# Moving the pieces of the modulation rows between the stages of a transformer layer on one core

## The chip, the cores and the metric

The kernel runs on one core of a Trainium2 chip. The metric is the time of one execution on the device in microseconds (us); the time before is the median of three runs. Engines are named as the profile names them: PE is TensorE's matmul, PEld its weight load, DVE is VectorE, ACT is ScalarE, POOL is GpSimd, and SP is SyncE, whose instruction stream issues nearly all loads.

## What is computed

One layer of a diffusion backbone: 256 latent tokens and 256 context tokens of width 2048, all in float32. Cut to what matters here:

```
m_lat = split(silu(c) @ w_ada + b_ada, 6)          # 6 modulation rows of 2048
m_ctx = split(silu(c_ctx) @ w_ada + b_ada, 6)      # of which 0 and 1 are used
h  = rms_norm(x,   norm1_g) * (1 + m_lat[1]) + m_lat[0]
hc = rms_norm(ctx, norm1_g) * (1 + m_ctx[1]) + m_ctx[0]
p, pc = h @ w_in, hc @ w_in[:, :3072]              # q, k, v and two gates; k, v alone for ctx
oa = grouped-query attention(rope(q_a), k_a, v_a)  # latent queries, all keys
ob = differential attention(rope(q_b), k_b, v_b)
merged = sigmoid(g_a) * (oa @ w_br_a) + sigmoid(g_b) * (ob @ w_br_b)
x1 = x + m_lat[2] * (merged @ w_out)
h2 = rms_norm(x1, norm2_g) * (1 + m_lat[4]) + m_lat[3]
out = x1 + m_lat[5] * ((silu(h2 @ w_ff_gate) * (h2 @ w_ff_up)) @ w_ff_down)
```

Rows 0 and 1 of the modulation are made early by matmuls (`ada_cond`). Rows 2, 4 and 3 (the gate, scale and shift around the second norm) and row 5 are made on VectorE in pieces, and the change concerns the first three of these.

## The kernel before

**Matmuls in three parts.** Weights and activations are split into a high and a low half. A weight tile is 128 x 2 x 512 (512 KB): SP loads it into a `wraw` buffer (seven of them), ScalarE casts it to `whi` (L235), VectorE makes `wlo` = raw - high (L237); three `whi` and three `wlo` buffers exist. `mm3` then issues activation-high by `whi` (L241), activation-high by `wlo` (L242) and activation-low by `whi` (L243). All engines run their instructions in the order in which they stand.

**Stages.** The projection to keys and values is done in channel steps, `STEPS = ((0, 1), (1, 1), (2, 2), (4, 4), (8, 4), (12, 4))`: first channel tile and number of channel tiles. The document names a step by its entry. Each step takes six column groups of 512; a group of the last three steps has two halves of one weight tile and 24 matmuls each, and at its end VectorE adds the four tokens' results to the sum in SBUF (L443). The last group of a step is `va` (column group 1). While a step runs, `ada_cond` makes rows 0 and 1 of the modulation for the next step: its weight pieces (`ada_t`) are loaded into `wraw` and other buffers (L295, L300, L304), and TensorE multiplies them in bursts (L315). `modulated` then makes the next step's activations: a product on VectorE (`hx`, L357), the high half on ScalarE (L360), the low half on VectorE (L361).

Then come the attention (q projections, gates, one branch projection, both attentions, woven together), the merge (`w_br_a`, 32 weight tiles), the output projection (`w_out`, 32 tiles), the feed-forward part.

**The pieces.** `ada_later` makes rows 2, 4 and 3, one after the other, each from 32 pieces: SP loads 512 KB of `w_ada` into a `wraw` buffer (L453), and VectorE multiplies it by the condition and adds it to an accumulator (L458 for the first two, L460 for the others). The accumulate of a piece is issued when the next piece is taken, and stands behind the last `wlo` issued by then. After 32 pieces four small matmuls sum the accumulator over the partitions (`adac`, L474), VectorE adds the bias (L475; for the scale it multiplies by `norm2_g`, L477), and POOL writes the row to DRAM (L478). `take(later, n)` takes n pieces; where these calls stand decides beside which work the pieces run. In the projection they stand in the loop over groups and halves, in the attention in `side_work`, which is called once per weight tile, in the merge after each of the last four weight tiles of a column group.

The order of instructions on an engine is settled when the program is built: a scheduler takes them by priority, which is the order of the code, and by when it thinks that their inputs and buffers are ready.

## Time and profile before

| what | value |
|---|---|
| median of three runs | 1694.38 us (1694.19 to 1694.4) |
| the profiled execution, its own time | 1696.49 us |
| its span, first to last instruction | 1694.7 us |
| mean granted clock of TensorE | 0.999 |
| VectorE: `wlo` (L237) | 607.0 us in 498 instructions |
| VectorE: pieces (L460, all rows) | 152.1 us in 120 instructions |
| HBM read | 395.35 MB, 243 GB/s over the span with writes |

A row of the timeline gives the start in us, the duration, engine, line, operation, what is written from what, the count, and in brackets how long the engine idled before it and who ended that. A row of a stretch gives its bounds, its length, the busy time of PE, PEld, DVE, ACT and POOL with their counts, the granted clock, the DMA share and GB/s. A row of the waits gives who waited for whom: us in total, times, the longest. On TensorE a matmul of 512 columns lasts 0.39 us, while the next one starts 0.23 us after it.

### The profile page before, as it was taken

To read this page: it belongs to the slowest core of one execution; us is meant where nothing else is said; L and a number is where in the kernel's file an instruction comes from. 1 tells how busy PE (TensorE), PEld (TensorE's weight loads), DVE (VectorE), ACT (ScalarE), POOL (GpSimd) and SP (SyncE) were. 2 spreads that over 40 slices of the span, in tenths; PEclk is the share of its full clock that TensorE was granted. 3 is DMA by queue.
4 is the path that set the end of the run, shared out by engine and by line. 5 is a ranking of instruction groups with operands and counts; after the bars stand their busy time and mean duration, and the time that the engine had idled before them with its cause. 6 is when DMAs were issued, how large, how long until landed. Compare 5 with 4: busy or idle time off the path is not lost.

```text
span 1694.7 us, 21499 instructions
## 1 busy us (share of the span) xinstructions
PE 1675.7 (99%) x7889; PEld 1354.8 (80%) x7889; DVE 1143.0 (67%) x1454; ACT 776.4 (46%) x1055; POOL 202.3 (12%) x296
## 2 busy tenths in 40 slices
PE   7999999999999999999999999999999999999998
PEld 5677778887887778888888888888888888888887
DVE  5765779697798888986666755566666666544454
ACT  5231222246666566667544534444444444333332
POOL 0200002011131110011111101111111111100000
PEclk9999999999999999999999999999999999999999
DMA  9888875777767767766877857888888898866662
GB/s 349 300 311 286 299 256 169 237 249 257 231 198 228 247 208 256 265 228 201 266 257 248 293 171 215 250 258 263 266 265 268 263 277 253 240 216 197 214 208 88
DMA packets 181284, 413.08 MB, mean 244 GB/s; under 512 B 15001, under 2 KB 16234, under 8 KB 180922
## 3 DMA queue, kind: packets, MB, share of 16 engines
q1 hardware_dynamic: 168906, 374.17, 67.3%
q0 software_dynamic: 12272, 37.53, 7.4%
q8 instruction: 62, 1.02, 0.3%
q14 instruction: 44, 0.36, 0.1%
HBM read 395.35 MB, written 16.29 MB: 243 GB/s over the span
## 4 chain that ended last, share of the span: by engine, by line
PE 92%; DVE 3%; DMA 2%; ACT 1%; issue 1%; POOL 0%; SPq 0%; DVEq 0%; ACTq 0%; POOLq 0%
PE mm L242 28%; PE mm L241 28%; PE mm L243 28%; PE ada L315 2%; PE ptp L815 1%; DVE wlo L237 1%; PE s L791 1%; PE mm L402 1%; PE o L836 1%; DMA wada<-in_ada_t_dram 1%; DMA wraw<-in_w_ff_gate_dram 0%; ACT whi L235 0%; DMA gate_d<-gate 0%; DMA wraw<-in_w_in_dram 0%; DVE ada L460 0%
## 5 line engine op out<-in xcount | busy, mean ns | idle before, releaser
L237 DVE TENSOR_TENSOR wlo<-wraw,whi 128x1024 fp32r<-128x1024 f32 x498 | 607.0, 1220 | 425.1 <-ACT whi L235 423.8
L235 ACT CAST whi<-wraw 128x1024 fp32r<-128x1024 f32 x498 | 522.8, 1051 | 727.1 <-PE mm L243 624.0
L242 PE MATMUL mm<-wlo,hT 128*128 128x512 f32 x684 | 266.2, 389 | 0.4 <-DVE wlo L237 0.4
L243 PE MATMUL mm<-whi,hT 128*128 128x512 f32 x684 | 266.1, 389 | 0.0
L241 PE MATMUL mm<-whi,hT 128*128 128x512 f32 x684 | 266.1, 389 | 0.0
L241 PE MATMUL mm<-whi,xT 128*128 128x512 f32 x630 | 251.9, 402 | 0.0
L242 PE MATMUL mm<-wlo,xT 128*128 128x512 f32 x630 | 247.3, 393 | 2.7 <-DVE wlo L237 2.7
L243 PE MATMUL mm<-whi,xT 128*128 128x512 f32 x630 | 246.8, 392 | 0.0
L460 DVE SCALAR_TENSOR_TENSOR ada<-wada,vt,ada 128x1024 f32<-128x1024 f32 x120 | 152.1, 1278 | 0.0
L242 PEld LDWEIGHTS mm<-wlo,hT 128*128 128x128 f32 x684 | 128.4, 188 | 27.7 <-DVE wlo L237 0.9
L241 PEld LDWEIGHTS mm<-whi,hT 128*128 128x128 f32 x684 | 128.4, 188 | 26.8
L243 PEld LDWEIGHTS mm<-whi,hT 128*128 128x128 f32 x684 | 128.4, 188 | 26.4
L241 PEld LDWEIGHTS mm<-whi,xT 128*128 128x128 f32 x630 | 118.2, 188 | 33.0 <-issue 6.6
L242 PEld LDWEIGHTS mm<-wlo,xT 128*128 128x128 f32 x630 | 118.8, 189 | 27.6 <-DVE wlo L237 5.0
L243 PEld LDWEIGHTS mm<-whi,xT 128*128 128x128 f32 x630 | 118.5, 188 | 25.8 <-DVE xT L361 0.3
L241 PE MATMUL mm<-whi,fT 128*128 128x512 f32 x354 | 137.5, 388 | 0.5 <-DVE y L1128 0.5
L242 PE MATMUL mm<-wlo,fT 128*128 128x512 f32 x354 | 137.3, 388 | 0.0
L243 PE MATMUL mm<-whi,fT 128*128 128x512 f32 x354 | 137.3, 388 | 0.0
L241 PEld LDWEIGHTS mm<-whi,fT 128*128 128x128 f32 x354 | 66.4, 188 | 15.0 <-issue 0.8
L243 PEld LDWEIGHTS mm<-whi,fT 128*128 128x128 f32 x354 | 66.4, 188 | 13.8
L242 PEld LDWEIGHTS mm<-wlo,fT 128*128 128x128 f32 x354 | 66.4, 188 | 13.7
L241 PE MATMUL mm<-whi,oT 128*128 128x512 f32 x192 | 75.9, 396 | 0.0
(236 smaller groups left out, 2142.7 us busy)
## 6 DMA issues: line engine op xcount, KB each, us to landing
wraw<-in_w_in_dram SPq DMA_DIRECT2D x159, 512.0 KB, 4.9
wada<-in_w_ada_dram SPq DMA_DIRECT2D x128, 512.0 KB, 4.7
wraw<-in_w_ff_gate_dram SPq DMA_DIRECT2D x88, 512.0 KB, 4.6
wraw<-in_w_ff_up_dram SPq DMA_DIRECT2D x88, 512.0 KB, 5.2
wraw<-in_w_ff_down_dram SPq DMA_DIRECT2D x88, 512.0 KB, 4.7
wada<-in_ada_t_dram SPq DMA_DIRECT2D x56, 512.0 KB, 6.6
wraw<-in_w_br_a_dram SPq DMA_DIRECT2D x32, 512.0 KB, 5.0
wraw<-in_w_out_dram SPq DMA_DIRECT2D x32, 512.0 KB, 5.1
```

The lines of the kernel that those rows point to most:

```text
L235: last_hi.append(nc.scalar.copy(out=hi[:, 0:nk], in_=raw[:, 0:nk]))
L237: last_lo.append(nc.vector.tensor_tensor(out=lo[:, 0:nk], in0=raw[:, 0:nk], in1=hi[:, 0:nk].bitcast(F32), op=ALU.subtract))
L241: nc.tensor.matmul(ps, lhsT=ah, rhs=wh, start=first, stop=False, skip_group_check=skip)
L242: nc.tensor.matmul(ps, lhsT=ah, rhs=wl, start=False, stop=False, skip_group_check=skip)
L243: return nc.tensor.matmul(ps, lhsT=al, rhs=wh, start=False, stop=last, skip_group_check=skip)
L315: last_pe[0] = nc.tensor.matmul(aps[32 * g:32 * g + 32, 0:ncol], lhsT=cst[:, k, :], rhs=rhs, start=k in first_ks, stop=k in last_ks)
L402: last_pe[0] = nc.tensor.matmul(ps[cg], lhsT=x, rhs=ws0[cg][y], start=(n == 0), stop=(n == 2))
L460: nc.vector.scalar_tensor_tensor(out=dst, in0=wt, scalar=sc[:, 0, kt:kt + 1], in1=dst, op0=ALU.mult, op1=ALU.add)
L791: nc.tensor.matmul(sps[i], lhsT=qT[rows, x, hh, tk * P:(tk + 1) * P], rhs=kT["b", grp][y][rows, hh, :], start=(n == 0), stop=(n == 2))
L815: nc.tensor.transpose(out=tp[:, kt * P:(kt + 1) * P], in_=p[:, kt * P:(kt + 1) * P], identity=ident)
L836: nc.tensor.matmul(op[:, 0:BV], lhsT=pT[:, kt, :], rhs=vb[:, kt, hh * BV:(hh + 1) * BV], start=(kt == 0), stop=(kt == 3))
```

## The change

Four things are edited.

- In `ada_cond`, the matmuls for the step (4, 4) run in the order in which their pieces were loaded, where they ran in reverse.
- In the projection, step (4, 4) takes a piece in every half of its first four groups too (two pieces per half in its last two, as before); step (8, 4) takes one per half in its first two groups and two per half in the other four, where it took one; step (12, 4) takes one per group, where it took one per half.
- In the attention, one of three calls of `side_work` takes a piece; it was one of two until the keys of branch a are made, and two of three after.
- The merge takes its pieces as its code did before, and there now are some left for it; the output projection takes a few at places of its first groups; the rest of `ada_later`, with the sum of the shift's row, and the broadcast of that row over the partitions (`b_all`) stand at the beginning of its third column group, where they stood before the output projection.

```diff
-                first_ks, last_ks = (range(0, 4), range(12, 16)) if k0 == 0 else (range(4, 8), range(8, 12)) if k0 == 4 else (range(12, 16), range(0, 4))
-                for k, rhs in held[::-1] if k0 else held:
+                first_ks, last_ks = (range(0, 4), range(12, 16)) if k0 in (0, 4) else (range(12, 16), range(0, 4))
+                for k, rhs in held if k0 in (0, 4) else held[::-1]:
...
-                if si == 3 and n >= 4:
-                    take(later, 2)
-                elif si > 3:
+                if si in (3, 4):
+                    take(later, 2 if n >= (4 if si == 3 else 2) else 1)
+                elif si == 5 and half == 0:
                     take(later, 1)
...
-            take(later, 1 if turns[0] % (3 if a_done else 2) else 0)
+            take(later, 1 if turns[0] % 3 == 0 else 0)
...
-    drain(later)
-    b_all = ada_everywhere("b_all", 2)
...
     for cg in range(4):
-        drain(project(w_out, mT, NKT, cg * CG, out_evac(cg), **(dict(tail=TURN2, hook=tail_hook, in_big=(6, 7)) if cg == 3 else {})))
+        if cg == 2:
+            drain(later)
+            b_all = ada_everywhere("b_all", 2)
+        for k, _ in enumerate(project(w_out, mT, NKT, cg * CG, out_evac(cg), **(dict(tail=TURN2, hook=tail_hook, in_big=(6, 7)) if cg == 3 else {}))):
+            if k in (2, 5, 6) and (cg or k > 4):
+                take(later, 1)
```

Since the scheduler weaves the engines' streams anew, the order of other instructions moves too. Three places on VectorE follow. `lo` stands for the low half of a weight tile; the rows are a line of the code, an operation, what is written from what, and the shape.

**First place: VectorE at the start of step (8, 4).** Before, from the first weight tile's low half of the new step (`wlo`, first row) to the third of the four adds on `va` that end step (4, 4):

```order
L237 TENSOR_TENSOR wlo<-wraw,whi 128x1024
L335 SCALAR_TENSOR_TENSOR mod_1484<-mod_1484,vt 128x8
L206 TENSOR_REDUCE lam<-used 128x2
L357 SCALAR_TENSOR_TENSOR hx<-tok_t_1040,mod_1484,r_all 128x256 x6
L361 SCALAR_TENSOR_TENSOR xT_1490<-hx,mod_1256,xT_1490 128x256 x4
L443 TENSOR_TENSOR va_102<-mm,va_102 128x512
L361 SCALAR_TENSOR_TENSOR cT<-hx,mod_1256,cT 128x256
L443 TENSOR_TENSOR va_102<-mm,va_102 128x512
L361 SCALAR_TENSOR_TENSOR cT<-hx,mod_1256,cT 128x256
L357 SCALAR_TENSOR_TENSOR hx<-tok_t_1040,mod_1484,r_all 128x256
L443 TENSOR_TENSOR va_102<-mm,va_102 128x512
```

Now VectorE has, from the second of those four adds to that same first `wlo` of step (8, 4):

```order
L443 TENSOR_TENSOR va_102<-mm,va_102 128x512
L357 SCALAR_TENSOR_TENSOR hx<-tok_t_1040,mod_1508,r_all 128x256 x2
L443 TENSOR_TENSOR va_102<-mm,va_102 128x512
L361 SCALAR_TENSOR_TENSOR cT<-hx,mod_1268,cT 128x256
L443 TENSOR_TENSOR va_102<-mm,va_102 128x512
L361 SCALAR_TENSOR_TENSOR cT<-hx,mod_1268,cT 128x256
L357 SCALAR_TENSOR_TENSOR hx<-tok_t_1040,mod_1508,r_all 128x256
L206 TENSOR_REDUCE lam<-used 128x2
L237 TENSOR_TENSOR wlo<-wraw,whi 128x1024
```

The `wlo` stood ahead of the new step's activations and of all four adds; it now stands behind the fourth add and one instruction each of L361, L357 and L206. On TensorE, four L241 of the new step stand ahead of its first L242, where it was one.

**Second place: VectorE at the start of step (12, 4).** Before, from that step's first `wlo` to the third add on `va` of step (8, 4):

```order
L237 TENSOR_TENSOR wlo<-wraw,whi 128x1024
L335 SCALAR_TENSOR_TENSOR mod_2103<-mod_2103,vt 128x8
L460 SCALAR_TENSOR_TENSOR ada_1433<-wada_2195,vt,ada_1433 128x1024
L357 SCALAR_TENSOR_TENSOR hx<-tok_t_1598,mod_2103,r_all 128x256 x3
L361 SCALAR_TENSOR_TENSOR xT_2109<-hx,mod_1869,xT_2109 128x256 x3
L357 SCALAR_TENSOR_TENSOR hx<-tok_t_1598,mod_2103,r_all 128x256 x4
L443 TENSOR_TENSOR va_102<-mm,va_102 128x512
L361 SCALAR_TENSOR_TENSOR xT_2109<-hx,mod_1869,xT_2109 128x256
L361 SCALAR_TENSOR_TENSOR cT<-hx,mod_1869,cT 128x256
L443 TENSOR_TENSOR va_102<-mm,va_102 128x512
```

Now VectorE has, from a piece just ahead of the four adds to the step's first `wlo` and the piece behind it:

```order
L460 SCALAR_TENSOR_TENSOR ada_2209<-wada_2250,vt,ada_2209 128x1024
L443 TENSOR_TENSOR va_102<-mm,va_102 128x512 x2
L357 SCALAR_TENSOR_TENSOR hx<-tok_t_1622,mod_2147,r_all 128x256
L443 TENSOR_TENSOR va_102<-mm,va_102 128x512
L361 SCALAR_TENSOR_TENSOR cT<-hx,mod_1893,cT 128x256
L443 TENSOR_TENSOR va_102<-mm,va_102 128x512
L357 SCALAR_TENSOR_TENSOR hx<-tok_t_1622,mod_2147,r_all 128x256 x3
L361 SCALAR_TENSOR_TENSOR cT<-hx,mod_1893,cT 128x256 x3
L237 TENSOR_TENSOR wlo<-wraw,whi 128x1024
L460 SCALAR_TENSOR_TENSOR ada_2209<-wada_2253,vt,ada_2209 128x1024
```

The `wlo` moved from ahead of the activations to behind the fourth add and three instructions each of L357 and L361. TensorE again has four L241 ahead of the first L242.

**Third place: VectorE in the attention, in the first q group of branch a.** The normalisation of the second token tile's q (`ss` to `nr`) stands ahead of a weight tile's `wlo`. Before, it ends so:

```order
L493 TENSOR_REDUCE ss<-sq 128x4
L502 TENSOR_TENSOR nr<-mm,rp_qa 128x512
L123 TENSOR_SCALAR rstd<-ss 128x4
L504 TENSOR_TENSOR sq<-mm,rp_qa 128x512
L460 SCALAR_TENSOR_TENSOR ada_5364<-wada_5700,vt,ada_5364 128x1024
L506 TENSOR_TENSOR nr<-nr,sq 128x4x64
L507 TENSOR_TENSOR nr<-nr,sq 128x4x64
L237 TENSOR_TENSOR wlo<-wraw,whi 128x1024
```

Now the same place on VectorE reads:

```order
L493 TENSOR_REDUCE ss<-sq 128x4
L741 RECIPROCAL rs<-rs 128x1
L502 TENSOR_TENSOR nr<-mm,rp_qa 128x512
L123 TENSOR_SCALAR rstd<-ss 128x4
L504 TENSOR_TENSOR sq<-mm,rp_qa 128x512
L237 TENSOR_TENSOR wlo<-wraw,whi 128x1024
L506 TENSOR_TENSOR nr<-nr,sq 128x4x64
L507 TENSOR_TENSOR nr<-nr,sq 128x4x64
```

The piece is gone and L506 and L507 moved behind the `wlo`. Some rows ahead of these, in the normalisation of the first token tile, L475 and L477 (bias and factor of the scale's row) were put in.

## The prediction

> **What bounds the kernel now.** I read the page's first and fourth part, then the waits of TensorE, then the stretches.

> ```profile
> PE 1675.7 (99%) x7889; PEld 1354.8 (80%) x7889; DVE 1143.0 (67%) x1454; ACT 776.4 (46%) x1055; POOL 202.3 (12%) x296
> PE 92%; DVE 3%; DMA 2%; ACT 1%; issue 1%; POOL 0%; SPq 0%; DVEq 0%; ACTq 0%; POOLq 0%
> PE ada L315 <- DMA wada<-in_ada_t_dram: 6.0, 2, 5.3
> PE mm L242 <- DVE wlo L237: 3.1, 4, 1.9
> 240.00:330.00 90.00, 90.00 (x410) 73.33 (x409) 76.07 (x109) 25.61 (x34) 11.23 (x6) 1.00 0.60 190
> 560.00:700.00 140.00, 137.45 (x656) 111.64 (x656) 119.58 (x175) 85.45 (x144) 15.21 (x16) 0.99 0.69 226
> ```

> TensorE is busy 99% of the span and makes 92% of the chain that ended last. The reader is to see how little there is to win: the fourth row says that in the whole run the matmul on a low half (L242) shows four waits on VectorE's `wlo` (L237), 3.1 us together. The last two rows (us, then busy us of PE, weight loads, DVE, ACT, POOL, clock, DMA, GB/s) show VectorE at 85% of the last third of the projection and of the middle of the attention: there VectorE, which issues in order, is the engine that TensorE nearly waits for. The change neither adds nor removes a matmul. So its worth is only this: which `wlo` comes late, and by how much.

> Two lines of TensorE's timeline show the worst one (start, us, instruction), and two stretches show what followed it:

> ```profile
> 625.81 0.39 PE L241 MATMUL mm<-whi,xT 128*128 128x512 f32 x1
> 628.05 0.50 PE L242 MATMUL mm<-wlo,xT 128*128 128x512 f32 x1 [1.86 <-DVE wlo L237]
> 625.80:629.10 3.30, 1.44 (x7) 0.87 (x6) 3.30 (x6) 0.59 (x1) 0.00 (x0) 1.00 0.51 148
> 629.20:632.60 3.40, 3.40 (x10) 2.65 (x9) 2.87 (x3) 0.37 (x1) 0.00 (x0) 0.50 0.80 234
> ```

> A matmul of 0.39 us is followed by the next after 0.23, so a wait costs 0.16 more than the idle time that is shown: 2.0 us here. After a stretch with PE busy 1.44 of 3.30 us the granted clock was 0.50 for 3.4 us, which lost half of that, 1.7 us.

> **The pieces, moved.** A piece costs VectorE this:

> ```profile
> 179.42 0.68 DVE L443 TENSOR_TENSOR va<-mm,va 128x512 f32<-128x512 f32 x1
> 180.02 0.15 DVE L208 TENSOR_TENSOR sums<-lam 128x1 f32<-128x1 f32 x1
> 180.09 1.28 DVE L460 SCALAR_TENSOR_TENSOR ada<-wada,vt,ada 128x1024 f32<-128x1024 f32 x1
> 181.28 0.48 DVE L361 SCALAR_TENSOR_TENSOR cT<-hx,mod,cT 128x256 fp32r<-128x256 f32 x1
> 184.07 1.22 DVE L237 TENSOR_TENSOR wlo<-wraw,whi 128x1024 fp32r<-128x1024 f32 x1
> ```

> From start to start a piece takes 1.19 us (180.09 to 181.28), an add 0.60. By the order of SP's loads the 96 pieces go from 32, 64, 0, 0 (projection, attention, merge, output) to 42, 36, 16, 2.

> **Term 1, the start of step (8, 4).** In the new order the first `wlo` of the step stands behind the last add of the step before (the first place shown with the change). That add waits for the last matmul of the old group, so what follows it cannot be early, whatever VectorE did before.

> ```profile
> 189.96 0.39 PE L241 MATMUL mm<-whi,xT 128*128 128x512 f32 x1
> 190.16 0.69 DVE L443 TENSOR_TENSOR kb<-mm,kb 128x512 f32<-128x512 f32 x1 [0.67 <-PE mm L243]
> 190.19 0.39 PE L242 MATMUL mm<-wlo,xT 128*128 128x512 f32 x1
> 171.16 0.28 DVE L206 TENSOR_REDUCE lam<-used 128x2 f32<-128x128 f32 x1
> 171.35 0.47 DVE L357 SCALAR_TENSOR_TENSOR hx<-tok_t,mod,r_all 128x256 f32<-128x256 f32 x1
> 245.23 1.27 DVE L357 SCALAR_TENSOR_TENSOR hx<-tok_t,mod,r_all 128x256 f32<-128x256 f32 x3
> 246.42 1.27 DVE L361 SCALAR_TENSOR_TENSOR xT<-hx,mod,xT 128x256 fp32r<-128x256 f32 x3
> ```

> A last add starts 0.20 us after the next group's first matmul (189.96, 190.16). Then, start to start: add 0.60, one L361 0.40 and one L357 0.40 (three L357 take 1.19, 245.23 to 246.42, and three L361 last as long), `lam` 0.19, and `wlo` 1.22 in full: 3.01 us. TensorE has four high-half matmuls (L241) ahead of the blocked L242 in the new order, 4 x 0.23 = 0.92 (189.96 to 190.19). Lost: **2.1 us**. An order forces this, so that a gain is excluded and little less is possible; it is up to 1 us more if VectorE reaches the add late.

> **Term 2, the start of step (12, 4).** Here three L357 and three L361 stand between the last add and the `wlo` (the second place): 0.20 + 0.60 + 1.19 + 1.19 + 1.22 = 4.40, less 0.92: **3.5 us**, up to 4.5 for the same reason. Nothing hides it: everything on TensorE stands behind that L242.

> **Term 3, loads in step (8, 4).** At the end of its third column group one weight tile lands just in time today:

> ```profile
> 206.93 1.05 ACT L235 CAST whi<-wraw 128x1024 fp32r<-128x1024 f32 x1 [7.14 <-DMA wraw<-in_w_in_dram]
> 209.49 1.05 ACT L235 CAST whi<-wraw 128x1024 fp32r<-128x1024 f32 x1 [1.51 <-DMA wraw<-in_w_in_dram]
> 208.01 1.23 DVE L237 TENSOR_TENSOR wlo<-wraw,whi 128x1024 fp32r<-128x1024 f32 x1 [2.49 <-ACT whi L235]
> 210.74 0.39 PE L242 MATMUL mm<-wlo,xT 128*128 128x512 f32 x1
> ```

> Its slack is 210.74 - 209.24 = 1.5 us. SP's queue holds it back behind the four half loads of L304, which wait for the conditioning matmuls. Now two pieces are loaded between those and the weight, and one less before them. Two loads land in 209.49 - 206.93 = 2.56 us, 1.28 each: the weight comes 1.3 to 2.6 us later, so 0 to 1.1 us late. The next three tiles, each with two pieces ahead of it and an accumulate that holds `wraw` buffers, are as near. I take **1.3 us** for the four; bounds 0 and 3.

> **Term 4, the clock.** The two waits of terms 1 and 2 are as long as the one at 625.81 or longer; whether one stretch holds enough of it depends on where it falls. I count one loss of **1.7 us**; bounds 0 and 3.4. [...]

> **Term 5, the attention.** The wait at 625.81 goes for the greater part. These steps of the chain of waits stand ahead of it:

> ```profile
> 625.00 1.19 DVE ada L460
> 626.19 0.34 DVE nr L506
> 626.53 0.34 DVE nr L507
> 626.86 1.15 DVE wlo L237
> 588.28 0.69 DVE L475 TENSOR_TENSOR adac_sb<-adac,adac_sb 128x512 f32<-128x512 f32 x1 [1.43 <-PE adac L474]
> 590.02 0.69 DVE L477 SCALAR_TENSOR_TENSOR adac_sb<-adac_sb,adac_g 128x512 f32<-128x512 f32 x1
> 613.93 1.23 DVE L237 TENSOR_TENSOR wlo<-wraw,whi 128x1024 fp32r<-128x1024 f32 x1 [1.73 <-ACT whi L235]
> ```

> The piece goes and L506 and L507 move behind the `wlo` (third place): 1.19 + 0.68 = 1.87 less. But the second row's L475 and L477, 0.6 each, come into the same stretch, so 0.67 net. Another piece, which held the tile before it by 1.19, moves into the idle 1.73 us ahead of 613.93. The wait of 2.0 falls by 0.7 to 1.9; I take 1.3, and with it the clock's 1.7 goes: **-3.0 us**, bounds -0.7 and -3.6. At 570 the same kind of wait loses its pieces:

> ```profile
> 567.98 1.27 DVE L460 SCALAR_TENSOR_TENSOR ada<-wada,vt,ada 128x1024 f32<-128x1024 f32 x1
> 571.77 0.50 PE L242 MATMUL mm<-wlo,xT 128*128 128x512 f32 x1 [0.56 <-DVE wlo L237]
> ```

> 0.56 + 0.16 = 0.7 lost there, and the accumulate ahead of that `wlo` moves behind it: **-0.7 us**; bounds -0.3 and -0.9.

> **Term 6, one new wait.** In the second q group of branch b the piece and L506, L507 now stand ahead of a `wlo` that they stood behind:

> ```profile
> 370.86 1.22 DVE L237 TENSOR_TENSOR wlo<-wraw,whi 128x1024 fp32r<-128x1024 f32 x1
> 372.66 1.28 DVE L460 SCALAR_TENSOR_TENSOR ada<-wada,vt,ada 128x1024 f32<-128x1024 f32 x1
> 372.91 0.40 PE L242 MATMUL mm<-wlo,xT 128*128 128x512 f32 x1
> ```

> That `wlo` ends at 372.08 and is used at 372.91. It comes 1.19 + 0.68 = 1.87 later (L506 and L507 at 0.34 each, as above): **1.0 us** late; bounds 0 and 1.0.

> **The merge and the output: nothing.** VectorE idles long enough per weight tile:

> ```profile
> 822.26 1.23 DVE L237 TENSOR_TENSOR wlo<-wraw,whi 128x1024 fp32r<-128x1024 f32 x1 [0.89 <-ACT whi L235]
> 824.98 1.23 DVE L237 TENSOR_TENSOR wlo<-wraw,whi 128x1024 fp32r<-128x1024 f32 x1 [1.50 <-ACT whi L235]
> ```

> 1.19 fits in 1.50. If a piece lands late, 1 us is lost; bounds 0 and 1. The shift's row now goes at the output's second column group, its four small matmuls move with it, and POOL's copy of it waits for one landing, well ahead of the norm that reads it two groups later.

> The conditioning's matmuls for step (4, 4) run in the order of loading instead of the reverse. The waits row of L315 holds two waits, 5.3 at the kernel's start and 0.7 at another step, and none here: nothing, bounds 0.7 either way.

> **The sum.** 2.1 + 3.5 + 1.3 + 1.7 - 3.0 - 0.7 + 1.0 = +5.9 us on the profiled execution's 1696.49 (span 1694.7, 1.8 around it): 1702.4. The median of the runs is 1694.38, 2.1 below that execution; I carry the difference over: **1700.3 us**.

> **Rivals.**
> 1. *No clock loss.* Terms 1 to 3 as above, but the waits split over two stretches: 1698.6. The row at 625.80 speaks against it: 1.86 us of waiting in one stretch was enough. [...]
> 2. *The relief in the attention wins* (faster). Place: the q norms at 566 to 632. Price: all of 2.0 + 1.7 + 0.7. It decides from the point where the boundaries together cost under 4.4 us, which needs terms 3, 4 and 6 at nothing and a shorter way from the add to `wlo` than the rows give. With the boundaries hidden whole: 1690.0. The order of VectorE speaks against it.
> 3. *They cancel.* Terms 1 and 2 at 5.6, the relief at its bounds, 3.6 and 0.9, the rest near 0: 1695.5.
> 4. *Loads starve.* Term 3 at 3 us, two clock losses, the relief half (-2.0): 1705. For it: the 7.14 us that ScalarE sat waiting for a weight at 206.93. Against it: the same two pieces per tile run today at the end of step (4, 4) without a wait.

> That the change doesn't move what it says is excluded by SP's order.

> **How the numbers follow.** Forecast 0.50, rival 1 0.16, rival 2 0.08, rival 3 0.14, rival 4 0.12. The range 1695.0 to 1704.5 takes in terms at their bounds singly and leaves out rival 2 and the worst of 4. About 0.2% (3.4 us) is what a measurement of this kernel can tell from no change. Slower: most of the forecast (0.48), 0.10 of rival 1, all of rival 4: 0.70. Within: the rest of those and rival 3: 0.22. Faster: 0.08.

> **What would show it.** After the change TensorE's waits should name L242 on `wlo` near 179 (about 2 us) and near 256 (about 3.5), each ended by L237 right behind an add on `va`; a stretch of clock 0.50 behind the second; no wait over 1.4 us near 630; a wait of about 1 near 378; none between 790 and 960. I am wrong if the boundary waits are below 4.4 us together, or if a weight's landing ends waits of more than 3 us in step (8, 4).

## The result and the profile after

| | before | after |
|---|---|---|
| time, median of 6 runs | 1694.39 us | 1704.83 us (1704.18 to 1708.12) |
| ratio to before | | 1.0065, interval 1.0052 to 1.0077 |
| profiled execution | 1696.49 us | 1704.18 us |
| its span | 1694.7 us | 1702.4 us |

The change makes the kernel slower, by 10.4 us in the medians and 7.7 us between the two profiled executions. The forecast was 1700.3; its range ended at 1704.5.

The page of after, its first part, as shown for before:

```profile
PE 1678.5 (99%) x7889; PEld 1354.7 (80%) x7889; DVE 1143.6 (67%) x1454; ACT 777.2 (46%) x1055; POOL 194.1 (11%) x296
```

The work is the same (7889 matmuls, VectorE's sum the same to 0.6 us). TensorE's share of the chain that ended last is 91%, one point lower than before; VectorE's and the DMA's are one point higher. What TensorE waited for (sum, times, longest, in us), without the waits at the kernel's start, which before has as well:

```profile
PE mm L242 <- DVE wlo L237: 6.0, 5, 3.0
PE o L836 <- DVE qT L247: 1.5, 1, 1.5
PE mm L241 <- DVE va L443: 0.8, 2, 0.4
```

The first row was 3.1, 4, 1.9. The second and third are new. And the stretch of the middle of the attention, with the columns as in the prediction:

```profile
560.00:700.00 140.00, 138.51 (x680) 113.16 (x679) 107.29 (x165) 88.09 (x149) 12.80 (x16) 1.00 0.62 196
```

VectorE is at 77% there (107.29 of 140), where it was at 85%, so the relief came. It was paid for elsewhere.

To see where, I matched the matmuls of L241, L242 and L243 (with those of L402, 6822 in each trace) one by one and took the difference of their starts. The three sums of a modulation row that stand at another place in the program (L474, 1.09 us each) are taken out. Each number is good to about 0.2 us, by where the border between two places is drawn:

```
place in the span, us              later than before by, us
start to 58                        -0.6   (the first load)
60 to 134, conditioning            +0.9
137, a late weight in step (4, 4)  +1.3
180 to 185, start of step (8, 4)   +3.1
185 to 255, steps (8, 4)           +2.1   (late low halves, 0.3 to 0.6 each)
261, start of step (12, 4)         +3.5
265 to 340, the clock              +1.8
340 to 566                         +0.2
570 and 590                        +0.7   (-0.7 and +1.4)
625 to 665                         -3.9   (the wait and its clock loss)
695 to the end                     -1.4
sum                                +7.7
```

Everything that the change costs stands in the first 340 us, and 1.4 us at 590. The merge and the output, with 16 and 2 pieces, show no wait between 790 and 960.

**The start of step (8, 4).** TensorE's timeline of after, then the cast of the step's first weight tile on ScalarE and rows of VectorE's timeline (start, us, instruction, idle time before it and what ended it):

```profile
180.80 0.61 PE L241 MATMUL mm<-whi,xT 128*128 128x512 f32 x2
181.75 0.47 PE L241 MATMUL mm<-whi,cT 128*128 128x512 f32 x1 [0.33 <-DVE va L443]
182.65 0.50 PE L241 MATMUL mm<-whi,cT 128*128 128x512 f32 x1 [0.43 <-DVE va L443]
184.76 0.50 PE L242 MATMUL mm<-wlo,xT 128*128 128x512 f32 x1 [1.61 <-DVE wlo L237]
```

```profile
172.69 1.05 ACT L235 CAST whi<-wraw 128x1024 fp32r<-128x1024 f32 x1 [3.92 <-DMA wraw<-in_w_in_dram]
180.93 0.67 DVE L443 TENSOR_TENSOR va<-mm,va 128x512 f32<-128x512 f32 x1
181.92 0.67 DVE L443 TENSOR_TENSOR va<-mm,va 128x512 f32<-128x512 f32 x1
183.31 0.27 DVE L206 TENSOR_REDUCE lam<-used 128x2 f32<-128x128 f32 x1
183.51 1.20 DVE L237 TENSOR_TENSOR wlo<-wraw,whi 128x1024 fp32r<-128x1024 f32 x1
```

The wait is where term 1 put it, behind the last add on `va`. But that add starts 1.12 us after the new group's first matmul (180.80 to 181.92), not 0.20: VectorE was at the activations and the earlier adds until then. Two of the four L241 wait for those adds as well, since they write accumulators that the adds still read (0.33 and 0.43 us of idle time, ended by L443). Together 3.1 us, where the term had 2.1. The weight itself was not late: its high half was ready at 173.74, almost ten us before the `wlo` starts. It is the order on VectorE that held the low half back.

**The start of step (12, 4).** The same views:

```profile
260.76 0.61 PE L241 MATMUL mm<-whi,xT 128*128 128x512 f32 x2
265.21 0.80 PE L242 MATMUL mm<-wlo,xT 128*128 128x512 f32 x1 [3.00 <-DVE wlo L237]
```

```profile
253.27 1.03 ACT L235 CAST whi<-wraw 128x1024 fp32r<-128x1024 f32 x1
260.96 0.69 DVE L443 TENSOR_TENSOR va<-mm,va 128x512 f32<-128x512 f32 x1 [0.28 <-PE mm L243]
261.57 1.27 DVE L357 SCALAR_TENSOR_TENSOR hx<-tok_t,mod,r_all 128x256 f32<-128x256 f32 x3
262.76 1.27 DVE L361 SCALAR_TENSOR_TENSOR cT<-hx,mod,cT 128x256 fp32r<-128x256 f32 x3
263.94 1.22 DVE L237 TENSOR_TENSOR wlo<-wraw,whi 128x1024 fp32r<-128x1024 f32 x1
```

Here VectorE sat idle before the add, which starts 0.20 us after the first matmul (260.76 to 260.96). The chain is add, three L357, three L361, `wlo`, as in term 2, and so is the cost, 3.5 us. Here too the high half was ready long before, at 254.30.

**A late weight.** In step (4, 4) SP now issues a weight (L224) behind the conditioning's half loads (L304) and a piece (L453); the weight lands late, ScalarE casts it late, and VectorE and TensorE sit idle (the timeline, in order of time over SP's queue and three engines):

```profile
124.83 1.95 SPq L304 DMA_DIRECT2D wada<-in_ada_t_dram  x4
126.82 0.45 SPq L453 DMA_DIRECT2D wada<-in_w_ada_dram  x1
127.31 0.45 SPq L224 DMA_DIRECT2D wraw<-in_w_in_dram  x1
...
136.19 1.05 ACT L235 CAST whi<-wraw 128x1024 fp32r<-128x1024 f32 x1 [7.48 <-DMA wraw<-in_w_in_dram]
137.28 1.22 DVE L237 TENSOR_TENSOR wlo<-wraw,whi 128x1024 fp32r<-128x1024 f32 x1 [4.20 <-ACT whi L235]
138.56 0.50 PE L242 MATMUL mm<-wlo,xT 128*128 128x512 f32 x1 [0.76 <-DVE wlo L237]
```

TensorE loses 1.3 us there, 0.35 at the L241 ahead and 0.95 at this L242. In before the load of the same weight tile is the first of the two in this row of SP's queue, 15 us sooner and ahead of the half loads (which stand at 124.52 there), and the tile is cast at 121.84:

```profile
112.22 2.29 SPq L224 DMA_DIRECT2D wraw<-in_w_in_dram  x2
```

So the piece at 126.82 is the smaller part of it: pieces now stand among the earlier weight loads too, at 112.61 and 115.34, and this weight has fallen behind the half loads. It is term 3's mechanism, one step ahead of where the term looked.

**The new wait at 590.** VectorE's timeline, then TensorE's:

```profile
588.70 1.23 DVE L237 TENSOR_TENSOR wlo<-wraw,whi 128x1024 fp32r<-128x1024 f32 x1 [0.58 <-ACT whi L235]
589.85 0.75 DVE L798 SCALAR_TENSOR_TENSOR p<-p,rs 128x512 f32<-128x512 f32 x1
590.51 0.69 DVE L247 TENSOR_TENSOR qT<-qtp,qT 128x512 fp32r<-128x512 f32 x1
```

```profile
591.25 1.16 PE L836 MATMUL o<-vb,pT 128*128 128x128 f32 x8 [1.49 <-DVE qT L247]
```

The low half of the transposed q (L247) now stands behind a weight's `wlo` that itself waits for ScalarE, and behind L798; in before it stood ahead of both. It is the pattern of the two step starts again, at a place that the prediction didn't look at.

### The profile page after: what moved, and what is told of

The parts are those of the page before. It is cut to its first block, busy times and chain, and to the rows that moved or that the text cites. A ratio compares the mean times of both kernels' runs of the same rounds, so it can differ in the third digit from the quotient of the medians.

```text
span 1702.4 us, 21501 instructions
## 1 busy us (share of the span) xinstructions
PE 1678.5 (99%) x7889; PEld 1354.7 (80%) x7889; DVE 1143.6 (67%) x1454; ACT 777.2 (46%) x1055; POOL 194.1 (11%) x296
## 4 chain that ended last, share of the span: by engine, by line
PE 91%; DVE 4%; DMA 3%; issue 1%; ACT 1%; POOL 0%; SPq 0%; DVEq 0%; ACTq 0%; POOLq 0%
PE mm L242 27%; PE mm L243 27%; PE mm L241 27%; PE ada L315 2%; DVE wlo L237 1%; PE ptp L815 1%; DMA wraw<-in_w_in_dram 1%; DMA wada<-in_ada_t_dram 1%; PE o L836 1%; PE s L791 1%; PE mm L402 1%; DVE ada L460 0%; PE s L241 0%; DMA wada<-in_w_ada_dram 0%; PE o L241 0%
## 5 line engine op out<-in xcount | busy, mean ns | idle before, releaser
L237 DVE TENSOR_TENSOR wlo<-wraw,whi 128x1024 fp32r<-128x1024 f32 x498 | 606.7, 1219 | 433.4 <-ACT whi L235 432.2
L235 ACT CAST whi<-wraw 128x1024 fp32r<-128x1024 f32 x498 | 523.2, 1051 | 745.1 <-PE mm L243 585.9
L242 PE MATMUL mm<-wlo,hT 128*128 128x512 f32 x684 | 266.1, 389 | 0.0
L241 PE MATMUL mm<-whi,hT 128*128 128x512 f32 x684 | 266.1, 389 | 0.0
L243 PE MATMUL mm<-whi,hT 128*128 128x512 f32 x684 | 266.1, 389 | 0.0
L242 PE MATMUL mm<-wlo,xT 128*128 128x512 f32 x630 | 248.0, 394 | 6.1 <-DVE wlo L237 6.0
L241 PE MATMUL mm<-whi,xT 128*128 128x512 f32 x630 | 251.0, 402 | 0.4 <-DVE kb L443 0.3
L243 PE MATMUL mm<-whi,xT 128*128 128x512 f32 x630 | 246.9, 392 | 0.0
L460 DVE SCALAR_TENSOR_TENSOR ada<-wada,vt,ada 128x1024 f32<-128x1024 f32 x120 | 151.7, 1276 | 2.5 <-DMA wada<-in_w_ada_dram 2.5
L243 PEld LDWEIGHTS mm<-whi,hT 128*128 128x128 f32 x684 | 128.4, 188 | 26.7
L242 PEld LDWEIGHTS mm<-wlo,hT 128*128 128x128 f32 x684 | 128.4, 188 | 26.6
L241 PEld LDWEIGHTS mm<-whi,hT 128*128 128x128 f32 x684 | 128.4, 188 | 26.5
L242 PEld LDWEIGHTS mm<-wlo,xT 128*128 128x128 f32 x630 | 119.0, 189 | 32.2 <-DVE wlo L237 8.8
L241 PEld LDWEIGHTS mm<-whi,xT 128*128 128x128 f32 x630 | 118.1, 188 | 33.1 <-issue 7.9
L243 PEld LDWEIGHTS mm<-whi,xT 128*128 128x128 f32 x630 | 118.7, 188 | 25.3 <-issue 0.2
L241 PE MATMUL mm<-whi,fT 128*128 128x512 f32 x354 | 137.5, 388 | 0.5 <-DVE y L1131 0.5
L243 PE MATMUL mm<-whi,fT 128*128 128x512 f32 x354 | 137.3, 388 | 0.0
L242 PE MATMUL mm<-wlo,fT 128*128 128x512 f32 x354 | 137.3, 388 | 0.0
L241 PEld LDWEIGHTS mm<-whi,fT 128*128 128x128 f32 x354 | 66.5, 188 | 15.1 <-issue 0.8
L243 PEld LDWEIGHTS mm<-whi,fT 128*128 128x128 f32 x354 | 66.5, 188 | 13.8
L242 PEld LDWEIGHTS mm<-wlo,fT 128*128 128x128 f32 x354 | 66.5, 188 | 13.6
L241 PE MATMUL mm<-whi,oT 128*128 128x512 f32 x192 | 76.0, 396 | 0.0
```

Of the source, the lines that this page charges most:

```text
L235: last_hi.append(nc.scalar.copy(out=hi[:, 0:nk], in_=raw[:, 0:nk]))
L237: last_lo.append(nc.vector.tensor_tensor(out=lo[:, 0:nk], in0=raw[:, 0:nk], in1=hi[:, 0:nk].bitcast(F32), op=ALU.subtract))
L241: nc.tensor.matmul(ps, lhsT=ah, rhs=wh, start=first, stop=False, skip_group_check=skip)
L242: nc.tensor.matmul(ps, lhsT=ah, rhs=wl, start=False, stop=False, skip_group_check=skip)
L243: return nc.tensor.matmul(ps, lhsT=al, rhs=wh, start=False, stop=last, skip_group_check=skip)
L460: nc.vector.scalar_tensor_tensor(out=dst, in0=wt, scalar=sc[:, 0, kt:kt + 1], in1=dst, op0=ALU.mult, op1=ALU.add)
```

## The experiments

Each kernel is compared with before on the same chip. "Theory 1" in most is that the waits come from the loads of the ten pieces that moved into the projection, and from the order of VectorE that goes with them; the rival is VectorE's amount of work.

**The kernel before again**, no edit.

> The kernel before, unchanged, for a second profiled execution. Theory 1 (the first profiled execution is 2.1 us above the median of the runs because the wait at 625.81 and the clock loss behind it are not in every execution): a profiled execution near the median, 1694.4, shows no stretch of clock 0.50 after that wait, or a shorter wait there. Theory 2 (the 2.1 us are somewhere else): the wait of 1.9 us and the clock loss of 1.7 us are there again, at the same place. Ratio to itself 1.000 either way.

Measured: 1694.45 us, ratio 1.0001 (0.9992 to 1.001); the profiled execution 1694.2. TensorE's waits between 340 and 790, and the two stretches at and behind the wait near 625:

```profile
PE mm L242 <- DVE wlo L237: 2.1, 2, 1.6
```

```profile
625.71:629.12 3.41, 1.79 (x8) 1.14 (x8) 3.41 (x6) 0.58 (x1) 0.00 (x0) 1.00 0.56 154
629.12:632.53 3.41, 3.41 (x20) 2.89 (x19) 3.41 (x5) 1.18 (x2) 0.00 (x0) 1.00 0.83 249
```

The wait is there again, 0.2 us shorter, but the clock behind it stays at 1.00. So the 1.7 us that the first profiled execution lost there are not in every execution; with 0.6 at another place (1340 us), also absent here, they make up about what it stood above the median, 2.1 us. Theory 1 holds.

**The projection's part alone**, in the kernel before.

```diff
-                if si == 3 and n >= 4:
-                    take(later, 2)
-                elif si > 3:
+                if si in (3, 4):
+                    take(later, 2 if n >= (4 if si == 3 else 2) else 1)
+                elif si == 5 and half == 0:
                     take(later, 1)
```

> The kernel before with the new piece counts in the projection's channel steps alone (42 pieces there, 54 at the old rate in the attention). By the trace of after, TensorE is 12.1 us later than before at 332 us of the span, 0.6 of it earlier at the start, so this part costs 12 to 13 us if the parts add up: 1706.4 to 1707.4. By the terms 1 to 4 of the prediction alone (8.6 us): 1703.0. If the slowdown were in the attention instead: under 1698.

Measured: 1709.45 us, ratio 1.0083 (1.0069 to 1.0097), 2.0 us above the upper end of what was expected. The waits at the two starts are those of after (2.12 and 3.51 us from one matmul to the next, as there), each with a clock loss behind it in this execution (mean clock 0.998, 0.999 in after with one loss), and the attention shows three new waits (1.2, 1.1 and 0.8 us near 521, 526 and 584) beside the one at 570. So the slowdown is in the projection, and the attention's part of the change gives some of it back.

**The attention's part alone**, in the kernel after: the projection's piece counts and the conditioning order are those of before, and the merge takes 24 pieces, since the projection keeps its 32.

```diff
-            if k > 3:
+            if k > 1:
                 take(later, 1)
```

> The kernel after with the old piece counts in the projection (32) and the old order of the conditioning matmuls; attention at the new low rate, 24 pieces in the merge (two more per column group) and 4 in the output. If the whole relief that the two traces show behind 560 us (4.4 us) is in the median as well: 1690.0. If 2.1 us of it were only in the profiled execution of before: 1692.1. If the merge can't take 24 pieces: 1694 or above.

Measured: 1698.26 us, ratio 1.0022 (1.0013 to 1.0031): a miss for both main cases; it is the third that came. Between 340 and 790 TensorE's one wait over 0.2 us is 1.2 on `qT`; its waits between 790 and 960:

```profile
PE mtp L975 <- DVE m L968: 1.4, 3, 0.6
PE mm L242 <- DVE wlo L237: 1.3, 4, 0.5
```

TensorE's matmuls at 781 us are 4.8 us ahead of before (1.0 of it from the kernel's start); by 966 all of it is lost. The merge takes 16 pieces without a wait (after) and not 24. The wait on `qT` comes with the attention's low rate, whatever the projection does.

**The conditioning order undone**: L311 and L312 of after as in before.

> The kernel after with the old order of the conditioning matmuls for step (4, 4). The traces put 0.9 us on that order (between 60 and 134 us of the span): 1703.9. If the order costs nothing, as the prediction took it: 1704.8.

Measured: 1707.13 us, ratio 1.0073 (1.006 to 1.0085), by the ratio between the two sets of runs of after (1.0065 above, 1.0074 below). In its trace the wait for a load at 61 us is there (1.7 us, 0.7 in before), and the burst of two conditioning matmuls that after puts ahead of an L242 at 87 us, 0.9 us, is not. The order costs nothing that these runs can tell.

**Step (4, 4) alone**, in the kernel before.

```diff
-                if si == 3 and n >= 4:
-                    take(later, 2)
+                if si == 3:
+                    take(later, 2 if n >= 4 else 1)
```

> The kernel before with the eight new pieces of step (4, 4) alone (40 pieces in the projection, 56 in the attention). Theory 1 (the order at the start of a step and the loads behind the conditioning halves): the wait at the start of step (8, 4) costs 3.1 us as in after, a weight that lands late near 137 costs 1.3, the start of step (12, 4) nothing, the clock behind the first wait 0 or 1.7: 1698.6 to 1700.3. Theory 2 (the waits come from VectorE's sum of work in steps (4, 4) and (8, 4)): with 10 fewer pieces than after no wait over 1 us at the start of step (8, 4), under 1696.

Measured: 1699.09 us, ratio 1.0027 (1.0018 to 1.0036). The start of step (8, 4) costs 3.0, the late weight near 137 costs 1.6, one near 217 0.8, one clock loss follows the first (mean clock 0.999); the start of step (12, 4) costs nothing. Theory 1: the start of a step is spoilt by the pieces of the step before it.

**The starts freed by other counts**: the same 42 pieces, but none in the last column group of steps (4, 4) and (8, 4), in the kernel after.

```diff
-                if si in (3, 4):
-                    take(later, 2 if n >= (4 if si == 3 else 2) else 1)
+                if si == 3 and n < 5:
+                    take(later, 2 if n > 1 else 1)
+                elif si == 4 and n < 5:
+                    take(later, 2)
```

> The kernel after with the same 42 pieces in the projection, but none in the last column group of steps (4, 4) and (8, 4) and two per half in the groups ahead of it, so that the first low half of steps (8, 4) and (12, 4) stands ahead of the last adds again. Theory 1 (the order at the two starts costs 3.1 and 3.5 us and one to two clock losses of 1.7): 1704.8 - 8.3 to 10.0 = 1694.8 to 1696.5. Theory 2 (VectorE is full, so the waits move into the groups that got denser): 1700 or more. Between them if denser groups starve weight loads.

Measured: 1704.18 us, ratio 1.0062 (1.0049 to 1.0075): no gain. TensorE's longest waits between 100 and 300, and ScalarE's timeline:

```profile
PE mm L241 <- ACT whi L235: 5.4, 2, 3.9
```

```profile
218.62 1.04 ACT L235 CAST whi<-wraw 128x1024 fp32r<-128x1024 f32 x1 [9.42 <-DMA wraw<-in_w_in_dram]
```

Both waits at the starts are gone (L242's waits on `wlo` come to 0.9 us in the whole run, none over 0.4). In their place ScalarE waited 9.4 us for a weight to land, and TensorE for it. Theory 2's number came out, but not by its mechanism: VectorE isn't full (busy 40.7 of the 60 us from 180 to 240); the denser groups starve the weight loads.

**The mix**: 32 pieces in the projection, 46 in the attention, 16 and 2 behind it. It is the kernel after with the projection's counts and the conditioning order of before, and

```diff
-            take(later, 1 if turns[0] % 3 == 0 else 0)
+            take(later, 1 if turns[0] % (2 if turns[0] <= 60 else 3) == 0 else 0)
```

> The pieces of before in the projection (32) and its conditioning order; in the attention every second turn up to turn 60, every third behind it (46 pieces), 16 in the merge, 2 in the output. If the relief behind 560 us is worth what the two traces show without the clock loss (0.7 + 2.0 - 1.5 at the new wait + 0.6 = 1.8 us): 1692.4. If the new wait on qT goes too, because the order differs: 1691. If a lower rate helps nothing because VectorE isn't what TensorE waits for there: 1694.2.

Measured: 1694.8 us, ratio 1.0006 (0.9997 to 1.0015): the same. The waits at 570, 590 and 625 are gone, but there are two others, 0.7 us at 349 and 1.4 at 375, where matmuls of L791 wait for ScalarE.

**The kernel after again**, no edit.

> The kernel after, unchanged, for a second profiled execution. The waits at the starts of steps (8, 4) and (12, 4) the same to 0.1 us (2.6 and 3.0 shown). Behind the second one clock loss of 1.7 us again; behind the first a loss in some executions only: with it about 1706.5, without it about 1704.5. If every loss belonged to a fixed place in the program: one loss, at 265, as in the first profile.

Measured: 1706.61 us, ratio 1.0074 (1.0061 to 1.0088). The stretches at and behind the two starts:

```profile
181.67:185.08 3.41, 1.37 (x4) 0.37 (x2) 3.41 (x8) 1.52 (x4) 0.00 (x0) 1.00 1.04 402
185.08:188.49 3.41, 2.98 (x7) 2.42 (x8) 3.41 (x7) 2.03 (x3) 0.75 (x1) 0.50 0.73 232
263.59:267.00 3.41, 0.62 (x2) 0.19 (x1) 3.41 (x8) 1.87 (x4) 0.00 (x0) 1.00 0.15 59
267.00:270.41 3.41, 3.09 (x7) 2.51 (x8) 3.41 (x4) 0.00 (x0) 0.00 (x0) 0.50 0.57 161
```

The waits are the same to 0.01 us, but this execution loses the clock behind both. The medians of the two sets of runs differ by 1.8 us, about what one loss costs.

**The mix with the odd turns**, so that VectorE's order is that of before up to about 555 us.

```diff
-            take(later, 1 if turns[0] % (2 if turns[0] <= 60 else 3) == 0 else 0)
+            take(later, turns[0] % 2 if turns[0] <= 60 else 1 if turns[0] % 3 == 0 else 0)
```

> As the mix before it, but with the pieces at the odd turns up to turn 60, which is where before has them, so that VectorE's order is that of before up to about 555 us and sparser behind it. Theory 1 (the two waits of the mix near 348 and 372, 3.0 us together, come from the even turns; the sparse stretch takes away 0.7 at 570 and 2.0 at 625): 1691. Theory 2 (a piece less in one place always makes something else on VectorE late): 1693.8, with a new wait of 1 us or more on another tile.

Measured: 1691.02 us, ratio 0.9984 (0.9975 to 0.9994): faster than before, by 3.1 us; that is little, but the interval leaves out 1. TensorE's waits between 340 and 790:

```profile
PE o L836 <- DVE qT L247: 0.4, 1, 0.4
```

That row is the whole answer for the attention; the waits of before (2.1 us in the second profile) and of the mix (348 and 372) are gone. Theory 1.

**No loads**: the first 42 pieces are summed from the identity, which is always in SBUF, so they need no DMA; otherwise the kernel after.

```diff
+            if n_piece[0] <= 42:
+                wt = ident.unsqueeze(1).to_broadcast([P, 8, P])
+            else:
                 wt = wp.tile([P, 1024], F32, tag="wraw", bufs=WRAW, name="wada2")
                 nc.sync.dma_start(out=wt, in_=w_ada[...])
```

> The kernel after without the loads of the first 42 pieces: VectorE sums as much, from a tile that is always there, so the output differs. Theory 1 (the ten pieces more cost by their loads: they hold the weights back, and by that set the order at the starts of the steps too): no late weight near 137 and 217, the first low half of steps (8, 4) and (12, 4) in time: 1704.8 to 1706.6 less 3.1, 3.5, 2.3, 1.3 and one or two clock losses of 1.7 = 1692.9. Theory 2 (they cost by VectorE's time): 1702 or more.

Measured: 1693.36 us, ratio 0.9998 (0.9989 to 1.0007). TensorE's waits between 100 and 300 (this one row is all), and the stretch from 130 to 180, of after and then of this kernel:

```profile
PE mm L241 <- DVE kb L443: 0.3, 1, 0.3
```

```profile
130.00:180.00 50.00, 49.14 (x235) 38.00 (x234) 37.34 (x54) 12.07 (x15) 0.00 (x0) 1.00 0.90 334
```

```profile
130.00:180.00 50.00, 50.00 (x241) 39.13 (x241) 38.61 (x58) 13.98 (x19) 0.00 (x0) 1.00 0.65 229
```

VectorE is as busy as in after (38.6 us of 50, 37.3 there), the DMA engines are at 65% for 90%, and no wait is left but 0.3. Theory 1: it is the loads, and with them the order at the starts.

**No sums**: the loads are there, but VectorE leaves out the sums of all but four of the 42; otherwise the kernel after.

```diff
+            skip = kt > 0 and n_piece[0] <= 42
             yield None
+            if skip:
+                continue
```

> The kernel after with all loads, but without VectorE's sums of the first 42 pieces (all but four of them), so the output differs. Theory 1 (the loads): the late weight near 137 stays (1.3), the start of step (12, 4) stays at 3.5 because the order there is the same, the start of step (8, 4) falls to 1 to 2; with one clock loss 1700 to 1703. Theory 2 (VectorE's time): all waits between 130 and 270 us go, 1693 to 1695.

Measured: 1696.85 us, ratio 1.0014 (1.0005 to 1.0022), between the two. The start of step (12, 4) still costs 1.8 us, that of step (8, 4) and the weight near 137 nothing. A piece's load holds one of the buffers that the weights use until VectorE has summed it; without the sum the buffer is free sooner, and the loads run ahead: the weight load that SP issues at 123.10 in after stands at 117.50 here, and the weight that was cast at 136.19 is cast at 134.76. So load and sum share the cost: the load takes the queue, and the sum sets how long it keeps the buffer. How much each has can't be told from these two.

**The first tile early**: the piece counts of after, but the first weight tile of steps (8, 4) and (12, 4) is loaded and split half a group earlier.

```diff
+    ahead = {}
     def kv_group(k0, nk, cg, first=False):
...
-        wt = {}
+        wt = {0: ahead.pop((k0, cg))} if (k0, cg) in ahead else {}
...
+                if si in (3, 4) and n == 5 and half == 0:
+                    ahead[steps[si + 1][0], 2] = load_w(w_in, steps[si + 1][0] * P, 2 * CG, WK)
```

> The kernel after with all its pieces where they are, but the first weight tile of steps (8, 4) and (12, 4) is asked for half a column group earlier, ahead of the pieces of the last half; its low half then stands ahead of the last adds. Theory 1 (the order at the two starts costs by itself what the traces show there): 3.1 and 3.5 us and the clock losses behind them (one or two of 1.7) go: 1704.8 to 1706.6 less 8.3 to 10.0 = 1696.5, with the late weights near 137 and 217 as before. Theory 2 (the loads of ten more pieces must be paid somewhere: with the starts freed a later weight lands late instead, as it did with the denser groups): 1701 or more, with a wait on whi or wlo of over 2 us near 205 to 220.

Measured: 1698.04 us, ratio 1.0018 (1.0009 to 1.0027), where after had 1.0065 and 1.0074: 8.0 to 9.5 us by the ratios. TensorE's waits between 100 and 300:

```profile
PE mm L242 <- DVE wlo L237: 2.1, 3, 0.8
```

The third of them is the late weight near 137. The other two:

```profile
187.70 0.50 PE L242 MATMUL mm<-wlo,xT 128*128 128x512 f32 x1 [0.53 <-DVE wlo L237]
254.70 0.50 PE L242 MATMUL mm<-wlo,xT 128*128 128x512 f32 x1 [0.82 <-DVE wlo L237]
```

Neither is at a start. Steps (8, 4) and (12, 4) begin at 180.66 and 259.37 here, and their first L242 waits for nothing; these are the second weight tile of step (8, 4) and a tile half a group ahead of step (12, 4). The profiled execution runs without a clock loss (mean clock 1.0). With not a piece taken away, the 3.1 and 3.5 us at the starts are gone, and 0.7 and 1.0 stand beside them instead. Theory 1: most of what the change costs is the order at the two starts, and the clock behind it.

## Why the prediction was off

The direction and the places were right: the two step starts, the late weights, the relief near 625. The measured median is 0.33 us above the range. Against the forecast of +5.9 on the profiled execution the traces show +7.7, and the rest of the miss of 4.5 us is in the step from there to the medians.

- **Carrying the difference over.** This step failed. "I carry the difference over" took 2.1 us off the sum, as if after would stand as far above its own median. But the 2.1 belong to before's profiled execution alone: a clock loss that the second one doesn't have, and 0.6 at 1340 us. After's profiled execution is 0.65 below its median. 2.75 us of the 4.5 are this. That the median ended only 0.33 us above the range is luck besides: the second set of runs has 1706.61. Put otherwise, term 5's 1.7 for the clock were a gain against one execution, not against the kernel.
- **Term 1** (2.1) was 3.1: the add was late by 0.9 more, since VectorE was behind, which the term's last sentence allowed for ("up to 1 us more") and the value didn't take.
- **Term 2** (3.5): 3.5. With VectorE idle ahead of the chain, the sum of its durations was the cost to 0.1 us. This and term 1 are shown by the early first tile, not only read.
- **Term 3** (1.3) was 2.1 in its own step, within its bounds, and the same mechanism cost 1.3 more in step (4, 4), which the term left out. That eight pieces were new there stands in the change; the landing of its weights was not looked at. Without the loads the whole of it goes.
- **Term 4** (1.7): one loss in the profiled execution, at the place named, two in the second execution. The bounds held; it isn't a number of the kernel but of an execution. Five profiled executions have the wait of 3 us at the first start (after twice, the projection's part, the conditioning order undone, step (4, 4) alone); four of them lost the clock behind it (mean clocks 0.999, 0.998, 0.998, 0.998 and 0.999 in this order; the first is the one without).
- **Term 5**: -3.9 at 625 for -3.0 (bound -3.6), mostly since all of the wait of 2.0 went and not 1.3 of it, and -0.7 at 570 as forecast. The new wait at 590, +1.4, was not foreseen. Its order stands in the program before any run: `qT` behind a `wlo`.
- **Term 6** (1.0) came as 0.2. The conditioning order, taken at nothing within 0.7, shows +0.9 in after's trace, and nothing in the medians when undone. Merge and output: nothing, as forecast, at 16 pieces; at 24, in the attention's part alone, the merge lost 4.8 us.

Rival 4 (loads starve) was the nearest in time, 1705, and in part in mechanism: late weights cost 1.3 us in step (4, 4) and 2.1 in step (8, 4), where it asked for 3 in the latter; two clock losses came in the second execution; but the relief came whole, not by half. Behind the two starts, too, it is the loads that set the order, as the kernel without them shows. Rival 2 (the relief wins) is what the mix with the odd turns shows: with no piece moved into the projection there is no start to pay for, and the relief stands alone, at 0.9984.

## What to carry to other kernels

When work is moved on an engine that issues in order (VectorE here started a `wlo` 9.8 us after its high half was ready, 173.74 to 183.51), look in the new order for every place where the first operand of the next group now stands behind the last result of the group before, on all engines and in every stage. Here each cost the chain from one to the other, 3.1 and 3.5 us, and loading the first operand earlier took it away at both places. A filler's load counted beside its arithmetic here (ratio 0.9998 without the loads, 1.0014 without the sums, 1.0065 and 1.0074 with both): it stood in the queue and in the buffers of the weights. Before a sum is made against one profiled execution, see whether the waits in it that had a clock loss behind them have it in a second one; the one near 625 had not.

## What the runs showed of the hardware

```profile
179.69:183.10 3.41, 2.65 (x10) 1.48 (x8) 3.41 (x8) 0.93 (x3) 0.00 (x0) 1.00 1.02 406
183.10:186.51 3.41, 1.80 (x9) 1.45 (x9) 3.41 (x7) 2.74 (x4) 0.75 (x1) 1.00 1.04 332
186.51:189.92 3.41, 3.41 (x17) 2.83 (x16) 3.39 (x4) 0.31 (x1) 0.00 (x0) 1.00 0.80 291
261.61:265.02 3.41, 0.50 (x1) 0.19 (x1) 3.41 (x8) 1.75 (x4) 0.00 (x0) 1.00 0.11 40
265.02:268.43 3.41, 3.22 (x8) 2.57 (x9) 3.41 (x4) 0.00 (x0) 0.00 (x0) 0.50 0.59 171
589.30:592.71 3.41, 1.92 (x13) 1.41 (x13) 3.41 (x5) 1.94 (x4) 0.00 (x0) 1.00 0.56 169
592.71:596.12 3.41, 3.41 (x18) 2.83 (x17) 1.90 (x4) 1.94 (x4) 0.56 (x1) 1.00 0.83 237
```

With TensorE busy for 0.50, 0.62, 1.37 and (in before, from 625.76) 1.55 us of a window the next 3.41 us ran at 0.50; with 1.79 (before again), 1.80, 1.92 and (without the sums, from 255.51) 2.01 they ran at 1.00. Between 1.55 and 1.79 these eight windows part. One window stands on the other side, in the kernel with the freed starts; a second one there, with 0.36 us busy, has the 6.83 us of clock 0.50 behind it:

```profile
136.95:140.36 3.41, 1.86 (x10) 1.10 (x8) 1.87 (x4) 1.04 (x1) 0.00 (x0) 1.00 1.04 399
140.36:143.77 3.41, 3.41 (x9) 2.62 (x9) 2.80 (x3) 1.05 (x1) 0.00 (x0) 0.50 0.98 384
215.45:218.86 3.41, 0.36 (x2) 0.00 (x0) 0.50 (x1) 0.23 (x1) 0.00 (x0) 1.00 1.03 405
218.86:225.69 6.83, 5.93 (x13) 4.24 (x14) 4.35 (x5) 1.85 (x2) 0.00 (x0) 0.50 1.03 387
```

So the same wait of 3.1 us at the start of step (8, 4) has 3.41 us at clock 0.50 behind it in one execution, where one window holds it (1.37 busy), and no stretch under 1.00 in another, where it is split over two (2.65 and 1.80 busy). Half of 3.41 is the 1.7 us by which I count a loss.
